# A hybrid decoder layer on one core: recurrence work moved between VectorE, ScalarE and GpSimd

## The chip, the cores and the metric

One core of a Trainium2 chip runs the whole kernel, a single launch. The metric is device time in microseconds (us) of one execution. The engines are TensorE (PE in the profile), VectorE (DVE), ScalarE (ACT), GpSimd (POOL) and SyncE (SP), which here only issues DMAs.

## What is computed

One inference step of one decoder layer, for 512 prompt tokens and 64 new tokens of 8 sampled sequences, 576 token columns in all. On the normalised input two mixers run side by side, a recurrent one (RWKV-7, 8 heads of 64) and a sparse attention (8 heads, 2 key/value heads); then gates, an output projection, a SwiGLU feed-forward network of width 2816 and a last normalisation. The change lies in the recurrent mixer, cut here to its core:

```python
def rwkv7_time_mix(p, prev_row, S0, lp):
    shifted = concat([prev_row[:, None, :], p[:, :-1]], axis=1)      # token shift
    xs = p + (shifted - p) * lp['mu']
    r, wlo, k, v, alo, glo = split(xs)
    w = -softplus(-(lp['w0'] + tanh(wlo) @ lp['w_decay'])) - 0.5
    decay = exp(-exp(w))
    a = sigmoid(lp['a0'] + alo @ lp['w_aaa'])
    kk = normalised(k * lp['k_k'])                                    # per head
    k_h = k * (1 + (a - 1) * lp['k_a'])
    y, S = rwkv7_scan(S0, r, decay, k_h, v, -kk, kk * a)
    ...
    return out, p[:, -1], S                                           # last row: the new shift state

def rwkv7_scan(S0, r, decay, k, v, a_vec, b_vec):                     # per token:
    S = S * w_t + (S @ a_t) b_t^T + v_t k_t^T ;  y_t = S @ r_t
```

## The kernel before

Tokens lie along the columns, features along the 128 partitions. Every projection in full precision is three TensorE passes: weights and activations are split into a rounded part (`whi`, `hh`) and a remainder (`wlo`, `hl`), and `mm3` (L354) adds hi·hi, hi·lo and lo·hi. ScalarE makes `whi` and VectorE makes `wlo` for each tile of 128 output columns (`wsplit`, L334), two buffers of each. A projection tile is 48 matmuls into two PSUM banks (`pd`), which ScalarE empties: into `pe` (L407) for a column tile of the recurrent mixer, into `nsp` or `gate` buffers for the rest.

The recurrent mixer works on four pairs of heads. For pair i, `shifted` makes the token-shifted tiles `k`, `r` and `v`: GpSimd subtracts neighbouring columns of `pe` (L411), VectorE corrects the samples' first columns from `shT` (L412) and blends (L413), and a copy of nine columns (L414) keeps the last rows for the output, in `so`. `rw_operands` makes decay sums and their exponentials (`th`, `cum`, `en`, `ec`, `em`), the normalised key (`kk`) and the in-context rate (`a`), and from them the operands of the chunks (`ag`, `bk`, `gb`, `bt`, all in the tile `state`). `rw_inverse` inverts triangular blocks by 15 elimination steps on VectorE (`invt`, `iw`) with DMAs on either side; `rw_merge_inverse` and `rw_fold_inverse` finish that with many small matmuls. `rw_chain` then walks 8 chunks of 64 tokens in order. For each chunk TensorE multiplies the state `sv` (L803, into `qy`), the state decayed by `lam` is made (`sl`, a slot of the tile `cct`, L806), VectorE copies the first product over `sv` (L807), TensorE multiplies again (L812) and VectorE adds product and decayed state into the next chunk's `sv`. `rw_samples` does the 8 sampled sequences.

Between these steps `pull` puts projection matmuls, so that TensorE has work while a pair's chain waits. The order of instructions on each engine is chosen by a scheduler from a model of the engines' times, with the chain at high priority; it is fixed when the kernel is built, and each engine then runs its own queue strictly in that order. So an edit of one instruction can move many others. After the recurrence come the attention heads (`ns_head`, with L1184, L1195 and L1199) and, from 660 us on, merge, output projection and feed-forward.

Of the kernel before, what the change touches and what calls it, by code (L numbers as in the profile page):

```python
# [16 lines left out]
AF = mybir.ActivationFunctionType  # L17
ALU = mybir.AluOpType
# [90 lines left out]
def tile_hybrid_step(ctx: ExitStack, tc: tile.TileContext, I: dict, O: dict):  # L109
# [3 lines left out]
    V = nc.vector  # L113
    A = nc.scalar
    G = nc.gpsimd
# [29 lines left out]
    def PS(tag, name="ps"):  # L145
        return psum.p.tile([128, 512], F32, name=nm(name), tag=f"b{next(banks[tag])}", bufs=1)
# [4 lines left out]
    def dma(out, in_, eng=None):  # L151
        (eng or nc.sync).dma_start(out, in_)  # L152

    def tt(e, out, a, b, op):
        return e.tensor_tensor(out, a, b, op)  # L155

    def bc(ap, shape):
        return ap.to_broadcast(shape)
# [9 lines left out]
    ident, vec, dvec, cst = base.t(128, "ident"), base.t(64, "vec"), base.t(16, "dvec"), base.t(4, "cst")  # L168
# [4 lines left out]
    def C(cols=NTOK, name="c", dt=F32):  # L173
        return base.t(592, name, "c", 3, dt)[:, 0:cols]
# [14 lines left out]
    def narrow(tag, name, cols=NTOK, dt=F32):  # L189
        p = held if tag in ("o4", "o5", "o6", "o7") else slots  # L190
        return p.t(NTOK, name, tag, 1, dt)[:, 0:cols]
# [11 lines left out]
    shT, so = base.t(15 * 8, "shT"), base.t(15 * 9, "so")  # L203
# [27 lines left out]
    V_W0, V_A0, V_KK, V_KA, V_RK, V_LNW, V_LNB = (31 + 4 * i for i in range(7))  # L231
# [29 lines left out]
    def vc(i):  # L261
        return vec[:, i:i + 1]
# [117 lines left out]
    def proj(pieces, evac):  # L380

        ws = ahead.pop(pieces[0][0], None) or wcols(w_in, pieces, raw=early.pop(pieces[0][0], None))
        for a in range(2):
            pt = PS("pd", "pd")
            for k in range(8):
                mm3(pt, ws[k:k + 1], hx[k:k + 1], cut(a), k == 0, k == 7)
                yield
            evac(cut(a), pt[:, 0:cut(a).stop - cut(a).start])
# [11 lines left out]
    def shifted(pieces, ti, new, then):  # L400
        pe = []

        def evac(c, pt):
            if not pe:
                pe.append(C(577, name="pe"))
                G.memset(pe[0][:, 0:1], 0.0)
            A.copy(pe[0][:, 1 + c.start:1 + c.stop], pt)  # L407
        yield from proj(pieces, evac)
        pe, x = pe[0], new()
        cur = pe[:, 1:577]  # L410
        tt(G, x, pe[:, 0:576], cur, ALU.subtract)  # L411
        tt(V, x[:, T:NTOK:8], shT[:, ti * 8:ti * 8 + 8], cur[:, T:NTOK:8], ALU.subtract)  # L412
        V.scalar_tensor_tensor(x, x, vc(16 + ti), cur, ALU.mult, ALU.add)  # L413
        V.tensor_copy(so[:, ti * 9:ti * 9 + 9], pe[:, 512:577:8])  # L414
        then(x, pe)

    def lora_decay(x, pe):
# [40 lines left out]
    def need(*key):  # L458
        while key not in have:
            pull(1)  # L460
        return have[key]
# [49 lines left out]
    def rw_operands(S, i):  # L511
        cols = slice(i * 128, i * 128 + 128)
        k = need("k", i)
        kk, k2 = narrow("o1", "kk"), narrow("o2", "k2")
# [4 lines left out]
        th, a = narrow("o3", "th"), narrow("o4", "a")  # L519
# [4 lines left out]
        for q, name in ((slice(0, 64), "rwkv_w_decay"), (slice(64, 128), "rwkv_w_aaa")):  # L524
            dma(raw[q], I[name][0][:, cols])
            c = slice(q.start * 2, q.start * 2 + 128)
            for q2 in (slice(0, 64), slice(64, 128)):
# [4 lines left out]
                 lambda c, z: A.activation(th[:, c], z, AF.Tanh, bias=dvec[:, i:i + 1], scale=0.5))  # L532
        small_mm([(w[:, 128:256], la), (w[:, 384:512], la)],
                 lambda c, z: A.activation(a[:, c], z, AF.Tanh, bias=dvec[:, 4 + i:5 + i], scale=0.5))
        G.tensor_scalar(th, th, 1.0, None, ALU.add)
        cum, en = narrow("o5", "cum"), narrow("o6", "en")
        V.tensor_tensor_scan(cum, scanm, th, 0.0, ALU.mult, ALU.add)
        tt(G, th, cum, th, ALU.subtract)
        G.tensor_scalar(a, a, 0.5, 0.5, ALU.mult, ALU.add)
        A.activation(en, cum, AF.Exp, scale=KAPPA)  # L540
        ec, em = cum, th
        A.activation(ec, cum, AF.Exp, scale=-KAPPA)
        A.activation(em, th, AF.Exp, scale=-KAPPA)
        G.tensor_scalar(kk, k, vc(V_KK + i), None, ALU.mult)
        A.activation(k2, k2, AF.Ln, scale=2.0 ** 20)
        A.activation(k2, k2, AF.Exp, bias=c_ln, scale=-0.5)
        tt(V, kk, kk, k2, ALU.mult)
        G.tensor_scalar(k2, a, vc(V_KA + i), dvec[:, 8 + i:9 + i], ALU.mult, ALU.add)
        kh, ba = k, a
        tt(G, kh, k2, k, ALU.mult)  # L550
        tt(G, ba, kk, a, ALU.mult)
# [13 lines left out]
        for h in range(2):  # L565
# [9 lines left out]
            lam = S["lam"][0:64, h]  # L575
# [194 lines left out]
    def gate_weights(i, after):  # L770
        cols = slice(i * 128, i * 128 + 128)
        wg, w1 = slots.t(256, "wgate", "wg1"), slots.t(128, "w1", dt=F32R)
        dma(wg[:, 0:128], I["rwkv_w_gate"][0][0:128, cols])
        dma(wg[0:32, 128:256], I["rwkv_w_gate"][0][128:160, cols])
        for q in (slice(0, 32), slice(32, 64)):
            behind(A.copy(w1[q], wg[0:32, 128:256]), after)
        tt(V, w1[64:96], wg[0:32, 128:256], f(w1[0:32]), ALU.subtract)
        G.memset(f(w1[96:128]), 0.0)
        return wg, w1

    def rw_chain(S, i):
        ag, gb, bt, sv, lam = (S[x] for x in ("ag", "gb", "bt", "sv", "lam"))
        par, ct = S["par"], S["ct"]
        G.memset(sv[0:64, 0], 0.0)
        yb = S["yb"].rearrange("p (j x) -> p j x", x=128)

        cct = slots.t(640, "cct", f"cc{par}")
        ccs = cycle([cct[:, x * 128:x * 128 + 128] for x in range(5)])

        def cc(name):  # L790
            return next(ccs)

        def two(ap):
            return ap.rearrange("p (h i) -> p h i", i=64)

        for c in range(8):
            if c == 4:
                wg, w1 = gate_weights(i, out)

            qy = PS(ct, f"qy{i}c{c}")  # L800
            with tc.high_priority():
                for h in range(2):
                    i_ = MM(qy[:, h * 64:h * 64 + 64], lhsT=ag[h][:, c], rhs=sv[:, c, h], start=h == 0, stop=True, skip_group_check=True)  # L803
                sl = cc("sl")
                sl3 = two(sl[0:64])
                tt(G, sl3, sv[0:64, c], bc(lam[0:64, :, c:c + 1], [64, 2, 64]), ALU.mult)  # L806
                V.tensor_copy(sv[0:64, c], two(qy[0:64, 0:128]))  # L807
            anchor[0] = i_
            pull(PULL[i])
            with tc.high_priority():  # L810
                for h in range(2):
                    i_ = MM(qy[:, 128 + h * 64:192 + h * 64], lhsT=S["btgb"][:, c, h], rhs=sv[:, c, h], start=False, stop=True,  # L812
                            skip_group_check=True)
                pn = two(qy[0:64, 128:256])
                if c < 7:
                    tt(V, sv[0:64, c + 1], pn, sl3, ALU.add)
                else:
                    fin = cc(f"fin{i}")
                    tt(V, two(fin[0:64]), pn, sl3, ALU.add)
                yo = yb[(c % 2) * 64:(c % 2) * 64 + 64, c // 2]  # L820
                out = A.copy(yo, qy[64:128, 0:128])
                tt(V, yo, qy[64:128, 128:256], yo, ALU.add)
            anchor[0] = i_
            pull(PULL[i])
        rw_samples(S, i)

        pf = PS(ct)
        TR(pf[:, 0:64], fin[0:64], ident[0:64, 0:64])
        fo = cc("fo")
        A.copy(fo[:, 0:64], pf[:, 0:64])  # L830
        dma(O["p_rwkv"][0, 0][2 * i:2 * i + 2].rearrange("h i j -> (h i) j"), fo[:, 0:64])

        st = slots.t(32, "gnst", "gnst", 2)
        y3 = yb.rearrange("p j (h i) -> p (j h) i", i=64)
        V.tensor_reduce(st[:, 0:10], y3, AX.X, ALU.add)
        V.tensor_scalar(st[:, 0:10], st[:, 0:10], -1.0 / 64, None, ALU.mult)
        tt(V, y3, y3, bc(st[:, 0:10, None], [128, 10, 64]), ALU.add)
        sq = slots.t(640, "gnsq", "ye")
        A.activation(sq.rearrange("p (j x) -> p j x", x=128), yb, AF.Square)
        V.tensor_reduce(st[:, 10:20], sq.rearrange("p (h i) -> p h i", i=64), AX.X, ALU.add)  # L840
        G.tensor_scalar(st[:, 10:20], st[:, 10:20], 1.0 / 64, GN_EPS, ALU.mult, ALU.add)
        tt(G, st[:, 20:30], st[:, 10:20], npow[:, 0:10], ALU.pow)
        tt(V, y3, y3, bc(st[:, 20:30, None], [128, 10, 64]), ALU.mult)

        p2, pt = PS(ct), PS(ct)
        TR(p2[:, 0:64], yb[0:64, 4], ident[0:64, 0:64])
        for j in range(4):
            TR(pt[:, j * 128:j * 128 + 128], yb[:, j], ident)
        y = slots.t(640, f"yT{i}", "ye")[:, 0:NTOK]
        A.activation(y[:, 0:T], pt, AF.Identity, bias=vc(V_LNB + i), scale=vc(V_LNW + i))  # L850
        A.activation(y[:, T:NTOK], p2[:, 0:64], AF.Identity, bias=vc(V_LNB + i), scale=vc(V_LNW + i))
        tt(G, y, y, yr[i], ALU.add)
        small_mm([(wg[:, 0:128], g0), (w1, g1)],
                 lambda c, pg: tt(V, yr[i][:, c], y[:, c], pg, ALU.mult), ct)
# [903 lines left out]
```

## Time and profile before

| | us |
|---|---|
| median of 3 runs | 1197.24 (1189.47 to 1200.94) |
| profiled execution, its own time | 1198.96 |
| its span, first to last instruction | 1197.2 |
| TensorE clock granted, mean share of full speed | 0.964 |

A profile is one execution. Busy time is the union of an engine's instructions. An idle time in brackets, [us <-who], is that of the engine just before the instruction, and whose result ended it. Lines such as L155 belong to helpers (a two-operand operation), so the tile names tell what an instruction is for. The granted clock is 1.00 at 2.4 GHz and 0.50 at 1.2 GHz.

### The profile page before, as it was taken

How to read it: one execution, taken by the hardware profiler on the slowest of the kernel's cores; microseconds unless marked ns; L12 is line 12 of the kernel's file. 1: busy time of each engine (PE TensorE's matmuls, PEld its weight loads, DVE VectorE, ACT ScalarE, POOL GpSimd, SP SyncE). 2: the span in 40 equal slices, each digit the busy share in tenths (PEclk: the TensorE clock that was granted, in tenths of full speed). 3: DMA queues.
4: the chain of work that ended last, by engine and by line, in shares of the span. 5: the costliest groups of instructions: out<-in, count | busy, mean ns of one | idle time of the engine just before them, and what ended most of it. 6: DMA issues, size and time to landing. Idle time of an engine off the chain costs nothing.

```text
span 1197.2 us, 23170 instructions
## 1 busy us (share of the span) xinstructions
PE 1139.2 (95%) x9117; PEld 1074.5 (90%) x9117; DVE 738.0 (62%) x1444; ACT 509.8 (43%) x1065; POOL 280.8 (23%) x361
## 2 busy tenths in 40 slices
PE   6989899999999989999999999999999999999995
PEld 5989799998888989777787899999999999999995
DVE  5684835359594561786668655698555763367554
ACT  5443533353433422576677433484223341233232
POOL 3443312146244131543237112201000010001000
PEclk9999999999987878999999999999999999999998
DMA  6323334212253242423240653313323243132222
GB/s 181 90 57 81 79 79 105 67 40 68 70 146 87 75 123 69 123 66 98 84 129 3 187 151 94 108 53 109 113 64 95 81 122 91 54 88 71 89 71 80
DMA packets 194791, 108.94 MB, mean 91 GB/s; under 512 B 49780, under 2 KB 187970, under 8 KB 194682
## 3 DMA queue, kind: packets, MB, share of 16 engines
q1 hardware_dynamic: 194682, 107.46, 32.0%
q8 instruction: 72, 1.18, 0.4%
q14 instruction: 37, 0.30, 0.1%
HBM read 91.40 MB, written 16.02 MB: 90 GB/s over the span
## 4 chain that ended last, share of the span: by engine, by line
PE 78%; DVE 11%; ACT 4%; issue 3%; DMA 2%; POOL 2%; SPq 1%; POOLq 0%; ACTq 0%; DVEq 0%
PE pd L359 46%; PE pu L359 9%; PE ps L704 2%; PE acc L1214 2%; PE ps L581 1%; PE ps L1035 1%; PE pT L1199 1%; DVE wlo L155 1%; PE ps L696 1%; PE pS L1184 1%; SPq L152 1%; DVE lo L155 1%; PE sm L396 1%; PE pTs L1308 1%; DMA vtok<-in_cache_slc_kv 1%
## 5 line engine op out<-in xcount | busy, mean ns | idle before, releaser
L359 PE MATMUL pd<-hh,whi 128*128 128x256 f32 (+1 forms) x656 | 206.2, 314 | 5.4 <-ACT pe L407 3.4
L359 PE MATMUL pd<-hh,wlo 128*128 128x256 f32 (+1 forms) x656 | 202.8, 309 | 5.1 <-DVE wlo L155 4.3
L359 PE MATMUL pd<-hl,whi 128*128 128x256 f32 (+1 forms) x656 | 202.7, 309 | 0.0
L359 PE MATMUL pd<-act,hi 128*128 128x288 f32 (+2 forms) x704 | 141.8, 296 | 0.0
L359 PEld LDWEIGHTS pd<-hh,whi 128*128 128x128 f32 x656 | 129.9, 198 | 8.8 <-ACT pe L407 4.4
L359 PEld LDWEIGHTS pd<-hh,wlo 128*128 128x128 f32 x656 | 129.9, 198 | 6.9 <-DVE wlo L155 4.6
L359 PEld LDWEIGHTS pd<-hl,whi 128*128 128x128 f32 x656 | 129.9, 198 | 1.4
L359 PEld LDWEIGHTS pd<-act,hi 128*128 128x128 f32 x704 | 112.6, 188 | 0.1
L359 PE MATMUL pd<-act,lo 128*128 128x288 f32 (+2 forms) x352 | 103.8, 296 | 0.0
L359 PE MATMUL pd<-h2l,hi 128*128 128x288 f32 x352 | 103.6, 295 | 0.0
L359 PE MATMUL pd<-h2h,hi 128*128 128x288 f32 x352 | 103.1, 295 | 0.0
L359 PE MATMUL pd<-h2h,lo 128*128 128x288 f32 x352 | 103.1, 294 | 0.0
L155 DVE TENSOR_TENSOR wlo<-wraw,whi 128x1024 fp32r<-128x1024 f32 x60 | 79.8, 1331 | 37.6 <-ACT whi L337 35.5
L337 ACT CAST whi<-wraw 128x1024 fp32r<-128x1024 f32 x59 | 61.8, 1047 | 93.5 <-PE pd L359 61.1
L155 POOL TENSOR_TENSOR sg<-sg,ut 128x576 f32<-128x576 f32 x11 | 18.1, 1645 | 340.0 <-DVE ut L155 325.3
L337 ACT CAST hi<-wraw 128x1024 fp32r<-128x1024 f32 (+1 forms) x46 | 46.5, 1012 | 117.4 <-PE pd L359 62.6
L155 DVE TENSOR_TENSOR x<-x,pd 128x288 f32<-128x288 f32 (+1 forms) x64 | 28.8, 451 | 65.2 <-PE pd L359 65.2
L155 DVE TENSOR_TENSOR lo<-wraw,hi 128x1024 fp32r<-128x1024 f32 (+1 forms) x46 | 56.9, 1239 | 18.7 <-ACT hi L337 18.6
L359 PEld LDWEIGHTS pd<-h2l,hi 128*128 128x128 f32 x352 | 66.1, 188 | 0.0
L359 PEld LDWEIGHTS pd<-act,lo 128*128 128x128 f32 x352 | 66.1, 188 | 0.0
L359 PEld LDWEIGHTS pd<-h2h,lo 128*128 128x128 f32 x352 | 66.0, 188 | 0.0
L359 PEld LDWEIGHTS pd<-h2h,hi 128*128 128x128 f32 x352 | 65.9, 188 | 0.0
(540 smaller groups left out, 2964.8 us busy)
## 6 DMA issues: line engine op xcount, KB each, us to landing
wraw<-in_w_in SPq DMA_DIRECT2D x35, 512.0 KB
wraw<-in_w_ffn_gate SPq DMA_DIRECT2D x22, 512.0 KB
ur<-in_w_ffn_up SPq DMA_DIRECT2D x44, 256.0 KB
wraw<-in_w_ffn_down SPq DMA_DIRECT2D x16, 512.0 KB
gt<-gsp SPq DMA_DIRECT2D x16, 288.0 KB
xt<-in_x_prompt SPq DMA_DIRECT2D x8, 512.0 KB
wraw<-in_w_out SPq DMA_DIRECT2D x8, 512.0 KB
wraw<-in_w_ffn_down SPq DMA_DIRECT2D x8, 384.0 KB
```

The source lines that it names most:

```text
L152: (eng or nc.sync).dma_start(out, in_)
L155: return e.tensor_tensor(out, a, b, op)
L337: e[0](hi[:, 0:n], raw[:, 0:n])
L359: i_ = MM(pt[:, 0:w_], lhsT=w, rhs=x[:, c], start=first and k == 0 and j == 0, stop=last and k == n - 1 and j == 2, **kw)
L396: MM(pt[:, 0:HALF], lhsT=l, rhs=r[:, half(a)], start=i == 0, stop=i == len(terms) - 1)
L581: MM(pt[:, c * 128:(c + 1) * 128], lhsT=bk[0:64, c0 + c], rhs=ag[:, c0 + c], start=True, stop=True)
L696: TR(pt[0:64, c * 128:c * 128 + 128], S["ag"][h][:, c0 + c, 0:64], ident)
L704: MM(pw[:, x * 64:x * 64 + 64], lhsT=S["at"][h][:, c], rhs=S["gb"][64:128, c, h], start=True, stop=True)
L1035: MM(po, lhsT=w[:, sl_], rhs=z[:, l, :, hf:hf + 162], start=hf == 0 and l == 0 and j == 0, stop=hf == 1 and l == 7 and j == 2)
L1184: MM(pS[:, 0:nk], lhsT=qs[:, qt * 128:qt * 128 + 128], rhs=kh[:, 0:nk], start=True, stop=False, skip_group_check=True)
L1199: TR(pT[:, kt * 128:kt * 128 + 128], P[:, kt * 128:kt * 128 + 128], ident)
L1214: MM(po[:, c0:hf * 256 + 256], lhsT=lv, rhs=ptx[m][:, kk * 256 + q0:kk * 256 + 256], start=name == "slc" and hf == 0 and kt == 0 and j == ...
```

## The change

Three moves between engines; the arithmetic stays the same. The decayed state `sl` of each chunk (32 instructions) goes from GpSimd to VectorE. Four scalings per pair of heads (16 instructions: `th` plus one, `a` to a half of itself plus a half, `k` times a column, `a` times a column plus a column) go from GpSimd to ScalarE. The 15 nine-column copies into `so` go from VectorE to ScalarE.

```diff
@@ shifted
         V.scalar_tensor_tensor(x, x, vc(16 + ti), cur, ALU.mult, ALU.add)
-        V.tensor_copy(so[:, ti * 9:ti * 9 + 9], pe[:, 512:577:8])
+        A.copy(so[:, ti * 9:ti * 9 + 9], pe[:, 512:577:8])
@@ rw_operands
-        G.tensor_scalar(th, th, 1.0, None, ALU.add)
+        A.activation(th, th, AF.Identity, bias=1.0)
...
-        G.tensor_scalar(a, a, 0.5, 0.5, ALU.mult, ALU.add)
+        A.activation(a, a, AF.Identity, bias=0.5, scale=0.5)
...
-        G.tensor_scalar(kk, k, vc(V_KK + i), None, ALU.mult)
+        A.mul(kk, k, vc(V_KK + i))
...
-        G.tensor_scalar(k2, a, vc(V_KA + i), dvec[:, 8 + i:9 + i], ALU.mult, ALU.add)
+        A.activation(k2, a, AF.Identity, bias=dvec[:, 8 + i:9 + i], scale=vc(V_KA + i))
@@ rw_chain
-                tt(G, sl3, sv[0:64, c], bc(lam[0:64, :, c:c + 1], [64, 2, 64]), ALU.mult)
+                tt(V, sl3, sv[0:64, c], bc(lam[0:64, :, c:c + 1], [64, 2, 64]), ALU.mult)
```

The scheduler makes a new order from it; up to the merge, every engine's queue is affected. Three places follow, before and then after.

ScalarE, first pair of heads, from the second half of `a` to the emptying of the next projection tile (`pe` from `pd_1008`; `whi_1167` are weights for a tile after it). Before:

```order
L534 ACTIVATE a_615<-sm_640,dvec_65 128x288
L528 CAST wl_1067<-wr_1066 64x128 x4
L540 ACTIVATE en_646<-cum_645 128x576
L337 CAST whi_1167<-wraw_1165 128x1024
L407 COPY pe_1005<-pd_1008 128x320
L542 ACTIVATE cum_645<-cum_645 128x576
L543 ACTIVATE th_614<-th_614 128x576
L407 COPY pe_1131<-pd_1045 128x256
```

After:

```order
L540 ACTIVATE en_646<-cum_645 128x576
L534 ACTIVATE a_615<-sm_640,dvec_65 128x288
L528 CAST wl_1067<-wr_1066 64x128 x4
L539 ACTIVATE a_615<-a_615 128x576
L542 ACTIVATE cum_645<-cum_645 128x576
L543 ACTIVATE th_614<-th_614 128x576
L548 ACTIVATE k_115_600<-a_615,dvec_65,vec_64 128x576
L337 CAST whi_1167<-wraw_1165 128x1024
L407 COPY pe_1005<-pd_1008 128x320
L414 COPY so_108<-pe_1005 128x9
L407 COPY pe_1131<-pd_1045 128x256
```

Between `en` and the emptying of `pd_1008` stood one cast; now a half of `a`, four small casts, two of the moved scalings and two exponentials stand there as well.

VectorE, around the end of the second pair's samples (`state` from `qy1c`, L752, which a matmul of the samples waits for), amid the elimination steps of the third pair. Before:

```order
L155 TENSOR_TENSOR iw_319<-iw_319,invt_3123 36x2x13x3
L155 TENSOR_TENSOR invt_3123<-iw_319,im_318 36x56
L155 TENSOR_TENSOR wlo_4404<-wraw_4401,whi_4403 128x1024
L155 TENSOR_TENSOR iw_319<-iw_319,invt_3123 36x2x14x2
L155 TENSOR_TENSOR state_317<-r_456_3352,cum_3958 64x4x64
L155 TENSOR_TENSOR state_317<-r_456_3352,cum_3958 64x5x64
L752 COPY state_317<-qy1c_500_3672 64x128
```

After:

```order
L155 TENSOR_TENSOR iw_319<-iw_319,invt_3123 36x2x12x4
L155 TENSOR_TENSOR wlo_4404<-wraw_4401,whi_4403 128x1024
L155 TENSOR_TENSOR invt_3123<-iw_319,im_318 36x78
L752 COPY state_317<-qy1c_500_3672 64x128
L155 TENSOR_TENSOR iw_319<-iw_319,invt_3123 36x2x13x3
```

The copy now stands ahead of the last two elimination steps and of the two products with `cum`.

GpSimd, from the spreading of the samples' queries (`qbr`, `qbu`) to the first attention probabilities (`P`). Before:

```order
L1116 TENSOR_SCALAR qbu_5898<-qraw_5894 64x8x8 x2
L778 MEMSET w_750_5509 32x128
L1116 TENSOR_SCALAR qbu_5898<-qraw_5896 64x8x8 x2
L155 TENSOR_TENSOR cct_5415<-state_317,lam_3911 64x128
L1195 TENSOR_SCALAR P_5927<-P_5927,ast_5237,gt_75 128x128
```

After:

```order
L1116 TENSOR_SCALAR qbu_5898<-qraw_5894 64x8x8 x2
L155 TENSOR_TENSOR yT_699_5048<-yT_699_5048,yr_81 128x576
L778 MEMSET w_750_5509 32x128
L1195 TENSOR_SCALAR P_5927<-P_5927,ast_5237,gt_75 128x128
L1195 TENSOR_SCALAR P_5940<-P_5940,ast_5237,gt_75 128x256
```

The decayed state has left the queue; the third pair's output sum `yT` has moved in front of the first probabilities, and the last two spreadings stand further back.

## Rows read from the trace of the kernel before

**Rows 1.** Page, engines: busy us (share of the span) and instructions.
```profile
PE 1139.2 (95%) x9117; PEld 1074.5 (90%) x9117; DVE 738.0 (62%) x1444; ACT 509.8 (43%) x1065; POOL 280.8 (23%) x361
```
**Rows 2.** TensorE's timeline: five matmuls that began after idle time, in brackets.
```profile
81.00 0.51 PE L396 MATMUL sm<-k,bones 128*128 128x288 f32 x1 [2.20 <-DVE k L554]
...
87.47 0.30 PE L562 MATMUL ps<-ident,v 128*64 128x128 f32 x1 [1.71 <-DVE yr L155]
...
146.81 0.39 PE L359 MATMUL pd<-hh,wlo 128*128 128x256 f32 x1 [4.34 <-DVE wlo L155]
...
342.23 0.36 PE L754 MATMUL qy1c<-state 64*64 64x64 f32 x1 [2.85 <-DVE state L752]
...
428.30 0.47 PE L812 MATMUL qy2c<-state 128*128 128x64 f32 x1 [3.29 <-DVE state L807]
```
**Rows 3.** Instruction groups by shape: count, busy us, mean ns, idle before, releaser.
```profile
L155 POOL TENSOR_TENSOR cct<-state,lam 64x128 f32<-64x128 f32 x32 | 19.2, 599 | 87.6 <-DVE state L155 78.8 <-PE ps L671 6.9 <-DVE so L414 1.3
L535 POOL TENSOR_SCALAR th<-th 128x576 f32<-128x576 f32 x4 | 7.4, 1859 | 15.2 <-ACT th L532 15.2
L544 POOL TENSOR_SCALAR kk<-k,vec 128x576 f32<-128x576 f32 x4 | 6.9, 1727 | 3.2 <-DVE k L413 3.2
L548 POOL TENSOR_SCALAR k<-a,vec,dvec 128x576 f32<-128x576 f32 x4 | 3.5, 879 | 0.3
L539 POOL TENSOR_SCALAR a<-a 128x576 f32<-128x576 f32 x4 | 3.5, 878 | 0.0
L1116 POOL TENSOR_SCALAR qbr<-qr 64x64 f32<-64x64 f32 x8 | 5.4, 675 | 0.5
L1116 POOL TENSOR_SCALAR qbu<-qraw 64x64 f32<-64x64 f32 x8 | 3.4, 421 | 0.5
L543 ACT ACTIVATE th<-th 128x576 f32<-128x576 f32 x4 | 2.7, 674 | 0.9 <-POOL th L155 0.9
L528 ACT CAST wl<-wr 64x128 fp32r<-64x128 f32 x16 | 4.7, 295 | 0.2
L414 DVE COPY so<-pe 128x9 f32<-128x9 f32 x15 | 12.3, 817 | 0.0
L807 DVE COPY state<-qy2c 64x128 f32<-64x128 f32 x8 | 2.3, 283 | 14.4 <-PE qy2c L803 14.3
L807 DVE COPY state<-qy0c 64x128 f32<-64x128 f32 x8 | 2.3, 282 | 5.5 <-PE qy0c L803 5.4
```
**Rows 4.** Timeline of the first pair's operands, 65 to 74 us.
```profile
65.99 1.12 DVE L414 COPY so<-pe 128x9 f32<-128x9 f32 x1
...
67.11 0.67 DVE L155 TENSOR_TENSOR v<-shT,pe 128x8 f32<-128x8 f32 x1
...
67.32 0.50 ACT L534 ACTIVATE a<-sm,dvec 128x288 f32<-128x288 f32 x1 [0.73 <-PE sm L396]
...
69.33 1.28 POOL L539 TENSOR_SCALAR a<-a 128x576 f32<-128x576 f32 x1
70.05 2.15 DVE L155 TENSOR_TENSOR wl<-wr,wl 64x128 fp32r<-64x128 f32 x2
70.17 0.69 ACT L540 ACTIVATE en<-cum 128x576 f32<-128x576 f32 x1 [1.23 <-DVE cum L537]
...
70.76 1.04 ACT L337 CAST whi<-wraw 128x1024 fp32r<-128x1024 f32 x1
71.70 0.42 ACT L407 COPY pe<-pd 128x320 f32<-128x320 f32 x1
...
73.25 0.35 ACT L407 COPY pe<-pd 128x256 f32<-128x256 f32 x1
```
**Rows 5.** Windows: stretch, length, busy us (count) per engine, clock, DMA share, GB/s.
```profile
342.00:348.80 6.80, 6.57 (x32) 6.46 (x32) 6.67 (x18) 1.75 (x3) 0.00 (x0) 0.50 0.77 214
...
376.10:400.00 23.90, 23.90 (x127) 21.38 (x128) 5.20 (x19) 6.75 (x15) 6.76 (x12) 0.50 0.13 29
400.00:427.30 27.30, 25.00 (x297) 24.10 (x295) 23.01 (x49) 11.47 (x26) 8.79 (x7) 1.00 0.42 112
```

## The prediction

> **What bounds the kernel now.** I read the engine table first: TensorE is busy for 95% of the span, and no edit touches its work [rows 1]. From 660 us to the end its projections run without a gap worth naming, so the change can only matter before. There I asked what TensorE waits for: its timeline, looking only at matmuls that begin after idle time. The five longest such waits between 60 and 498 us add up to 14.4 us (2.20 + 1.71 + 4.34 + 2.85 + 3.29), and all five end on VectorE [rows 2]. That is the first thing to see: VectorE, in the stretches where a pair's operands and inverse are made, is what is late; GpSimd matters as far as VectorE waits for it or is held up beside it. The second thing is the clock. For 23.9 us from 376 us on TensorE was granted 0.50, 1.2 GHz, and did 127 matmuls there, against 297 in the 27.3 us after it at 2.4 GHz; VectorE was busy for only 5.2 of those 23.9 us, so here TensorE's own slow clock was the limit [rows 5].
>
> **The decayed state** (32 instructions) leaves GpSimd, where one took 599 ns on average, and joins VectorE. A similar VectorE operation on 64x128, the copy at L807, takes 282 ns [rows 3], so 9.0 us of VectorE are added. On the path they cost nothing: the copy that follows waits for TensorE's product (L803) anyway, 14.4 us in eight chunks of the third pair, and in the first pair still 5.5 us in eight, 0.69 us a chunk, more than 0.28 [rows 3]. If that cover were gone the whole 9.0 us would show. The GpSimd version was seldom late, so I book 0, with -1 and +9 as ends.
>
> The rows show VectorE held up by GpSimd: two 64x128 operations took 2.15 us together beside two GpSimd instructions at 69 to 72 us [rows 4], where 0.28 each would do. The Trainium skill (SBUF — State Buffer, section Who interferes with whom) says that a VectorE instruction with two inputs in SBUF blocks wholly against a GpSimd instruction that reads SBUF; it speaks against this move, because the new product has two such inputs and the copy at L807 has only one, from PSUM. By that rule a part of the 32 would wait out a GpSimd instruction; the trace agrees that such holds exist, and the sum would rise by about 3 us, inside the ends above.
>
> **The nine-column copies** (15) took 12.3 us of VectorE, 817 ns each [rows 3], far more than nine columns need. The row at 65.99 shows why that is not a gain of 12: the copy ended at 67.11 and the next VectorE instruction, the correction of `v`, needs GpSimd's subtraction of the same tile, beside which the copy was held [rows 4]. Without the copy VectorE waits for that instead. I take -0.5, ends 0 and -3. ScalarE pays at most 0.3 us each, the price of a 64x128 cast [rows 3], 4.4 us beside other work.
>
> **The sixteen scalings** took 7.4 + 6.9 + 3.5 + 3.5 = 21.3 us of GpSimd. A ScalarE pass over the same 128x576 takes 674 ns (L543), so ScalarE gets 16 x 0.67 = 10.8 us [rows 3]. Of latency, `th` plus one (1.86 us down to 0.67) stands straight ahead of the decay sum, so that goes 1.2 us earlier in each pair. The other three only clear GpSimd's queue: the product with the scaled `a` comes no earlier, because ScalarE now makes that scaling at the end of a longer queue (below). VectorE is held less: L539 at 69.33 ran beside the slow pair of operations at 70.05 [rows 4]. I book -2 for that, ends 0 and -5, from the 1.6 us lost there (2.15 less twice 0.28), in up to three pairs.
>
> **Where TensorE's waits go.** The waits at 81.00 and 87.47 (3.9 us) end on VectorE work of the first pair. The decay sum comes 1.2 us sooner, the copy at L414 and a weight remainder no longer stand ahead of that work, and VectorE is held less: I let both waits go, -3.9. The wait at 146.81 (4.34) is a weight remainder queued behind elimination steps; the new order only moves the remainder that is late, 0. The wait at 342.23 (2.85) ends on L752, which now stands ahead of two elimination steps and two products: -2.3. For 428.30 (3.29), behind rotary work, I take -2.0: the order there changes, by an amount that I cannot see; its ends are 0 and -3.3 [rows 2].
>
> **What is paid for it.** On ScalarE the emptying of the next projection tile stood 1.53 us after the start of `en` (70.17 to 71.70). In the new order it stands behind half an `a` (0.5), four casts (4 x 0.3), four passes of 0.67 and the weight cast (1.0), with `en` itself 0.7 [rows 3, 4]: 6.1 us, so 4.6 us later, less the 1.2 us by which `en` starts sooner, 3.4. Queued behind it is TensorE, which needs that PSUM bank; it had work until the next emptying at 73.25, that is 1.5 us of cover. So it loses 1.9 us in the first pair, and in the other three I take a third of that each, as their queues differ: +3.8 in all; ends 0 and 4 x 3.4 = +13.6. On GpSimd, the first probabilities waited behind sixteen spreadings (5.4 + 3.4 us) [rows 3]; the decayed state leaves that queue and `yT` enters it ahead: +0.5 for TensorE, which waits for these probabilities either way.
>
> **The sum**, against the profiled execution's own 1198.96: 0 - 0.5 - 2 - 3.9 - 2.3 - 2.0 + 3.8 + 0.5 = -6.4, so 1192.6; the median shown is 1.7 lower than that execution, which is well inside the runs' spread. I predict 1192. A measurement of this kernel tells about 1%, 12 us, from no change.
>
> **Rivals.** First, *ScalarE's queue becomes the bound* (slower). At its upper end above, each pair stalls TensorE by 3.4 us with no cover, and the expected removals do not come, since VectorE's later steps wait for the same exponentials: 1199 + 13.6 = 1213. It decides from the point where the emptying is later than TensorE's other bank lasts, 1.5 us; for the first pair I already expect that, and against it stands that later pairs sit among small matmuls. Second, *the clock* (faster): if the new order keeps TensorE dense through the stretch at 376 to 400, up to half of 23.9 us comes back, and half of the 6.8 us from 342 on [rows 5]: 12 + 3.4 on top of the sum, 1177. Nothing in the edits aims at it, and it may as well go the other way. Third, *the waits only move*: the new queues put other instructions ahead of what TensorE needs, -6.4 comes to nothing, and the time is 1198. The wait at 146.81 is the model for it.
>
> The engine table alone would back this third one. PE is the busiest at 95%, and work goes from the idlest compute engine (POOL 23%) to busier ones, DVE 62% and ACT 43% [rows 1]. The Trainium skill (Perfetto Trace Analysis, section Identifying the Most-Contended Engine) says to optimize the engine with the highest occupancy first; by that rule this change gains nothing, 1199. The waits of rows 2 speak against taking the whole span at once.
>
> **How the numbers follow.** The forecast 0.46; the waits only move 0.20; ScalarE's queue 0.18; the clock 0.16. Of the forecast's own spread (the ends above, and one stretch of low clock more or less, 12 us either way) I put 0.14 below 1185 and 0.02 above 1209. Faster by over 1%: 0.16 + 0.14 = 0.30; slower by over 1%: 0.18 + 0.02 = 0.20; within 1%: 0.50. The range must reach both the clock's and the ScalarE queue's times to leave out 2 in 10: 1172 to 1213.
>
> **What would show it.** Right: no wait of TensorE on L554 or `yr` near 80 to 90 us; no wait on L752 near 340; a wait of 1 to 3 us on the emptying of `pe` (L407) near 75; the decayed state on VectorE at about 0.28 us with the copy L807 still waiting for TensorE; `so` at 0.3 us or less on ScalarE. Wrong: TensorE waiting on L407 or L337 in every pair, more than 5 us in all; new waits on VectorE longer than the five; or a sum of half-clock time that differs by over 20 us from before, which would outweigh all terms here.

## The result, and the profile after

The change made the kernel slower: 1211.85 us median (1209.34 to 1218.63, 4 runs) against 1198.31 (1189.47 to 1200.94), a ratio of 1.0129 with a 95% interval of 1.0087 to 1.0171. The forecast was 1192, range 1172 to 1213. The profiled execution took 1211.96 us, its span 1210.2, at a mean granted clock of 0.950 (0.964 before). Medians here and below are of all runs; the ratios leave out runs over 1.5% above the fastest of their kernel, and two experiments, in which most runs were such, have none.

What the edit does to the engines is as planned. Of the page after, the engines (answers to [rows 1]):

```profile
PE 1152.7 (95%) x9117; PEld 1087.0 (90%) x9117; DVE 729.4 (60%) x1461; ACT 523.3 (43%) x1096; POOL 242.2 (20%) x313
```

VectorE is busy for less time than before in spite of 17 more instructions (32 came, 15 left), GpSimd for 38.6 us less, and no engine but TensorE is near its limit. TensorE has the same 9117 matmuls, and they take 13.5 us longer. The moved instructions after answer to [rows 3]. The decayed state as a group by shape (columns as there):

```profile
L155 DVE TENSOR_TENSOR cct<-state,lam 64x128 f32<-64x128 f32 x32 | 9.0, 280 | 6.2 <-PE ps L671 5.6
```

The others by source line, with minimum, median and maximum in ns, and the first and last start:

```profile
L535 ACT ACTIVATE th<-th x4: 680/698/702, 64.8 to 321.2; 128x576 f32<-128x576 f32 x4
...
L539 ACT ACTIVATE a<-a x4: 667/682/687, 69.7 to 327.9; 128x576 f32<-128x576 f32 x4
...
L544 ACT ACTIVATE kk<-k,vec x4: 757/763/765, 54.2 to 281.5; 128x576 f32<-128x576 f32 x4
...
L548 ACT ACTIVATE k<-a,dvec,vec x4: 852/862/870, 71.4 to 328.7; 128x576 f32<-128x576 f32 x4
...
L414 ACT COPY so<-pe x15: 204/208/214, 30.5 to 286.8; 128x9 f32<-128x9 f32 x15
```

The prices of `sl`, `th` and `a` are close to those used; the scalings with a column for scale, or for scale and bias, took 0.76 and 0.86 us where 0.67 was used, the nine-column copies 0.21 of the 0.3 allowed. TensorE's timeline after, the matmuls that began after idle time where the prediction had looked (to set beside [rows 2]):

```profile
73.60 0.42 PE L359 MATMUL pd<-hh,whi 128*128 128x320 f32 x1 [0.92 <-ACT pe L407]
78.30 0.39 PE L359 MATMUL pd<-hh,wlo 128*128 128x256 f32 x1 [0.68 <-DVE wlo L155]
85.32 1.07 PE L562 MATMUL ps<-ident,v 128*64 128x128 f32 x8 [0.69 <-DVE yr L155]
...
131.61 0.64 PE L359 MATMUL pd<-hh,whi 128*128 128x320 f32 x1 [3.32 <-ACT nsp L887]
...
335.45 0.27 PE L828 MATMUL ps<-ident,cct 64*128 64x64 f32 x1 [2.08 <-DVE so L155]
...
416.57 0.20 PE L661 MATMUL ps<-invt,state 16*32 16x16 f32 x2 [2.03 <-DMA invt<-d2p]
...
497.39 0.66 PE L812 MATMUL qy3c<-state 128*128 128x64 f32 x4 [2.02 <-DVE state L807]
499.35 0.89 PE L1199 MATMUL pT<-ident,P 128*128 128x128 f32 x2 [0.89 <-DVE yr L155]
```

The waits for L554, L752 and the 4.34 us for `wlo` are gone, that for `yr` is shorter; others have come, and one at 497 stands where none of that length stood.

The decisive reading is a milestone. The first score product of the attention (L1184) comes at 498.9 us before and at 488.7 after, with the same work done on both sides but for twenty instructions in the order. So up to there the changed kernel is **10.2 us ahead** in these two profiles, and behind it it **lost 23**. Windows of the two heads, columns as in [rows 5], before and then after:

```profile
0.00:498.90 498.90, 466.62 (x4126) 435.76 (x4126) 293.74 (x591) 205.40 (x425) 165.97 (x214) 0.93 0.34 90
...
0.00:488.70 488.70, 462.95 (x4116) 433.73 (x4116) 282.42 (x604) 217.46 (x452) 124.91 (x166) 0.93 0.35 92
```

TensorE's idle time in the head (length less busy) fell by 6.5 us, from 32.3 to 25.8. The other 3.7 us are busy time, and no clear gain: some ten matmuls of the last pair's chain and gates now run behind the milestone, about 2 us by their spacing (an estimate). Nor does one profile tell 10 us here: with `sl` alone moved in the old order (below), a kernel whose time is that of before, the first L1184 came at 488.9 in an execution of 1188.83 us.

Windows from the first L1184 to the first turning of the selected pages' keys (L1284), and from there to the last product with the values (L1214); columns as in [rows 5]. Before:

```profile
498.90:547.60 48.70, 43.90 (x318) 35.02 (x318) 39.09 (x110) 34.44 (x104) 28.48 (x47) 0.93 0.30 73
547.60:664.00 116.40, 110.53 (x782) 89.50 (x781) 80.27 (x242) 78.11 (x253) 43.40 (x73) 0.99 0.26 79
```

After, the longest stretch at half clock first, then the two windows:

```profile
499.10:529.80 30.70, 30.45 (x153) 25.70 (x153) 14.51 (x45) 12.40 (x40) 10.65 (x17) 0.50 0.19 47
...
488.70:550.60 61.90, 55.59 (x306) 46.26 (x305) 38.37 (x105) 33.09 (x96) 28.62 (x45) 0.67 0.24 61
550.60:676.80 126.20, 115.93 (x808) 92.67 (x807) 83.33 (x249) 81.25 (x264) 45.28 (x75) 0.97 0.27 81
```

165.1 us before, 188.1 after, for the same work but for those matmuls. From there to the end both take the same time, 533.2 and 533.4 us. TensorE's idle time (length less busy) went from 10.7 to 16.6 us, its busy time from 154.4 to 171.5: some waits, and a clock that stood at 0.50 for 41 of the first 61.9 us (twice 0.33 of the length), 30.7 of them in one piece. None of the 63 moved instructions but the chain's last few stands in this stretch. What changed here is the order, which the scheduler had drawn anew.

### The profile page after: what moved, and what is told of

It is laid out like the page before. It is cut to its first block, busy times and chain, and to the rows that moved or that the text cites. A ratio compares the mean times of both kernels' runs of the same rounds, so it can differ in the third digit from the quotient of the medians.

```text
span 1210.2 us, 23174 instructions
## 1 busy us (share of the span) xinstructions
PE 1152.7 (95%) x9117; PEld 1087.0 (90%) x9117; DVE 729.4 (60%) x1461; ACT 523.3 (43%) x1096; POOL 242.2 (20%) x313
## 4 chain that ended last, share of the span: by engine, by line
PE 79%; DVE 8%; ACT 4%; DMA 4%; issue 2%; POOL 1%; SPq 1%; POOLq 0%; ACTq 0%; DVEq 0%
PE pd L359 47%; PE pu L359 9%; PE acc L1214 2%; PE ps L704 2%; PE ps L581 2%; PE pT L1199 1%; PE ps L1035 1%; PE pS L1184 1%; PE sm L396 1%; PE pq L733 1%; PE ps L696 1%; DVE lo L155 1%; DMA vtok<-in_cache_slc_kv 1%; PE pS L1186 1%; DVE wlo L155 1%
```

## The experiments

The order can be held fixed. The kernels below write the order of each engine out as a table of 11,444 numbers and give each instruction a dependency of order alone, with no wait, on the one that is to stand ahead of it:

```python
for n in seq:                                   # numbers in the order of the code
    i = traced[int(n)]
    e = str(i.engine).split(".")[-1]
    if e in last:
        tc.add_manual_dep(i, last[e].name, dep, reason="order of the engine's work")
    last[e] = i
```

So one can put new engines into an old order, cut between two orders, or move single queue entries. A moved instruction stands, in a foreign order, where it stood in time in that order.

**Engines against order: four runs.** Two theories: the new order costs the time, or the new engines do (ScalarE's queue).

`after_fixed`, the changed kernel with its own table:

```diff
         tile_hybrid_step(tc, ins, outs)
+        pin_order(tc, nc)          # table: the changed kernel's order
```

> The changed kernel with the order of every engine written out as it already was (dependencies of order alone, no wait), so that later runs can move single instructions. Both theories: 1212 us (1208 to 1219), the time of the changed kernel. If the low clock is set by the program, half-clock time is again about 120 us in all, with the long stretch from about 499 to 530 us; if it falls at random, its place is another one and the time may differ by 12 us either way.

1206.03 us (1196.41 to 1217.32, 10 runs), 1.0069 (1.0029 to 1.0110), less than the 1208 to 1219 expected. The profiled execution, 1204.8 us, has no long stretch of half clock behind L1184; that of `after_fixed_again` (below, the same program) has it, from 500.7 to 531.4 us, where the changed kernel had it. So the place is the same, and whether it comes differs between executions.

`new_engines_old_order`: the changed kernel, table of the kernel before.

```diff
+        pin_order(tc, nc)          # changed kernel; table: the order of before
```

> The moved instructions on their new engines, but every other instruction in the order of the kernel before, and the moved ones at the place in time that they had there. Theory 1 (the new order costs the time, through TensorE's stretch from 498 to 550 us and its low clock): 1190 to 1201, as before or a little less, half-clock time 70 to 100 us. Theory 2 (the engines cost it: ScalarE's longer queue and 9 us more of VectorE): 1206 to 1216.

1189.48 us, 0.9962 (0.9931 to 0.9993): faster than before, by a little more than expected. Theory 1.

`old_engines_new_order`: the kernel before, table of the changed kernel.

```diff
+        pin_order(tc, nc)          # kernel before; table: the changed kernel's order
```

> All instructions on the engines of before, in the order of the changed kernel. Theory 1 (order): 1206 to 1216, with a half-clock stretch of 20 us or more between 495 and 550 us. Theory 2 (engines): 1192 to 1201.

1209.01 us, 1.0110 (1.0041 to 1.0180): as slow as the changed kernel without one instruction moved between engines. Theory 1 in both corners: engines -0.4%, order +1.1%. The detail failed: its profile has some 14 us of half clock from L1184 to L1284 (clock 0.87 over 54.3 us), not a stretch of 20.

`after_late_gate`: the wait at 497, traced back, is VectorE's copy L807 behind a remainder of the gate weights, which waits for a cast, which waits for a transfer. Timeline of VectorE after:

```profile
496.74 0.28 DVE L155 TENSOR_TENSOR w<-wgate,w 32x128 fp32r<-32x128 f32 x1 [1.39 <-ACT w L776]
497.06 0.28 DVE L807 COPY state<-qy3c 64x128 f32<-64x128 f32 x1
```

Of ScalarE after:

```profile
496.41 0.62 ACT L776 CAST w<-wgate 32x128 fp32r<-32x128 f32 x2 [2.24 <-DMA wgate<-in_rwkv_w_gate]
```

```diff
-L776 CAST w<-wgate x2                 (ScalarE, ahead of chunk 6)
-L155 TENSOR_TENSOR w<-wgate,w         (VectorE, ahead of chunk 6's L807)
 L807 COPY state<-qy3c                 (chunk 7)
+L776 CAST w<-wgate x2
+L155 TENSOR_TENSOR w<-wgate,w
```

> The changed kernel in its own order, with three instructions moved back: the two casts of the last pair's gate weights on ScalarE (L776) and their remainder on VectorE now stand behind the copy of chunk 7 (L807) and not ahead of that of chunk 6, so that nothing waits for their transfer. The 2.0 us wait of TensorE at 497 goes in any case. Theory 1a (that wait is what is followed by 30 us at half clock): 1195 to 1201, half-clock time between 495 and 550 us under 15 us. Theory 1b (the clock falls in this stretch of small matmuls anyway): 1207 to 1212, and the half-clock stretch stays over 20 us.

1204.23 us, 1.0078 (1.0038 to 1.0118). It decides nothing, because the pause only moved. TensorE's timeline of this run:

```profile
496.67 0.66 PE L812 MATMUL qy3c<-state 128*128 128x64 f32 x4 [0.23 <-DVE state L807]
...
500.42 1.10 PE L1199 MATMUL pT<-ident,P 128*128 128x128 f32 x3 [2.55 <-DVE yr L155]
```

Then 0.50 from 500.2 to 530.9 us. The ten executions fall in two groups, six from 1199.5 to 1204.7 us at a mean clock of 0.955 to 0.961, four from 1212.1 to 1213.5 at 0.948 to 0.950.

**Where in the order: two cuts, and the edits apart.** `new_head_old_tail`: changed kernel, table of its own order to the first L1184, that of before behind it.

```diff
+        pin_order(tc, nc)          # table: new order up to L1184, then the order of before
```

> The changed kernel's engines throughout. Order of every engine: as in the changed kernel up to the first score product of the attention (L1184), which is reached with the same work done but for some twenty instructions, and as in the kernel before from there on. Theory 1c (the new order gains 7 to 10 us up to that point and loses 14 to 23 us behind it): 492 + 697 us of span, so 1186 to 1192 us, faster than before. Theory 1d (the head leaves something behind, so that any order is late behind it): 1200 to 1212.

1191.33 us, 0.9942 (0.9911 to 0.9974). Theory 1c.

`old_head_new_tail`, the reverse:

```diff
+        pin_order(tc, nc)          # table: order of before up to L1184, then the new one
```

> The same cut the other way: the order of before up to the first score product (L1184), the order of the changed kernel from there on, on the changed kernel's engines. Theory 1c: 496 + 711 to 721 us of span, so 1205 to 1219 us, and half-clock time behind the cut above 25 us in some executions. Theory 1d: 1188 to 1194.

1205.72 us, 1.0057 (1.0021 to 1.0093), with 27 us of half clock behind the cut in the profile. Theory 1c again: the loss is in the order behind L1184.

`sl_old_order` and `scalings_old_order`: one part of the change each, the order of before.

```diff
-                tt(G, sl3, sv[0:64, c], bc(lam[0:64, :, c:c + 1], [64, 2, 64]), ALU.mult)
+                tt(V, sl3, sv[0:64, c], bc(lam[0:64, :, c:c + 1], [64, 2, 64]), ALU.mult)
+        pin_order(tc, nc)          # table: the order of before
```

> Only the decayed state moves to VectorE, all else in the order of before. By the prediction's step (its cost is hidden behind TensorE's product): 1194 to 1197, no difference from before. By the rival step (9 us more of VectorE show): 1200 to 1205. If the state's way through the shorter VectorE instruction is the gain: 1189 to 1192.

1194.26 us, 0.9987 (0.9963 to 1.0011): no difference.

```diff
-        G.tensor_scalar(th, th, 1.0, None, ALU.add)
+        A.activation(th, th, AF.Identity, bias=1.0)
...
+        pin_order(tc, nc)          # the other three scalings too; table: the order of before
```

> Only the sixteen scalings move to ScalarE, all else in the order of before. If the gain of the new engines in the old order (0.4%) is mainly theirs (VectorE less held up, the decay sum earlier): 1189 to 1193. If ScalarE's queue takes it back: 1195 to 1201.

1188.71 us, 0.9929 (0.9896 to 0.9961). The gain of the new engines is the scalings'; the nine-column copies were not tried alone.

**The scheduler's own orders, and a third cut.** `sl_own_order` is the first of these two edits without the table:

```diff
-        pin_order(tc, nc)
```

> Only the decayed state moves to VectorE, in the order that the scheduler makes of it. With the order of before the same kernel took 0.9987 of the time of before, so what is different here is order alone. If any edit redraws the order and the time with it: outside 1190 to 1198. If the costly order comes from the changed kernel's scalings or copies: 1190 to 1198.

1211.59 us (1191.85 to 1218.71, 6 runs). The same edit cost nothing in the old order; here the spread alone is 27 us, and the median is that of the changed kernel. Its order behind L1184 is almost the changed kernel's: matched by line, tiles and shape in the traces, some 35 of VectorE's 857 instructions there stand elsewhere, against some 265 when it is compared with before. Its two windows (table below) are 49.4 and 125.3 us. So moving the decayed state alone makes the scheduler draw the costly tail. What that costs in all stays open here: one of the six ran at 1191.85.

`scalings_own_order`, likewise:

```diff
-        pin_order(tc, nc)
```

> Only the sixteen scalings move to ScalarE, in the scheduler's own order; with the order of before they gave 0.9929. If the scheduler's answer to the scalings is what costs: 1200 to 1212, with waits behind the first score product as in the changed kernel. If not: 1185 to 1193.

1193.25 us (1177.38 to 1203.27, 12 runs), 0.9947 (0.9908 to 0.9986). The scalings get an order of their own, unlike both others behind L1184, and it costs nothing measurable.

`new_order_to_pages`: cut at the first L1284.

```diff
+        pin_order(tc, nc)          # table: new order up to L1284, then the order of before
```

> The changed kernel with its own order up to the first turning of the selected pages' keys (L1284, about 542 to 550 us) and the order of before from there on; the cut at the first score product gave 1191, the order of the changed kernel throughout 1206 on the same chip. Theory 1e (about 6 us of the loss are waits behind this point, the rest is the wait for probabilities and low clock ahead of it): 1194 to 1203. If all of it lies ahead: 1204 to 1210. If all of it lies behind: 1189 to 1193.

1199.47 us, 1.0016 (0.9989 to 1.0042), as theory 1e has it: by the ratios some 9 us of the loss lie between the two cuts (0.9942 to 1.0016) and 6 behind the second (to 1.0069; 11 by the 1.0108 of the same program below).

`scalings_new_head_old_tail`, an attempt at a better version:

```diff
+        pin_order(tc, nc)          # scalings alone; table: new order up to L1184, then before
```

> A version that takes what gained: only the scalings move, the order of the changed kernel up to the first score product, that of before behind it. If the gains of engines and head add up: 1180 to 1188. If the head's gain is the same microseconds as the scalings': 1188 to 1192, as either alone.

1191.61 us, 0.9964 (0.9937 to 0.9992): faster than before, but the gains don't add up. The scalings in the old order have the lowest time of the versions tried, though not clear of noise: the intervals of all five that beat the kernel before overlap.

**Loads or compute queues.** `new_order_old_loads`:

```diff
+        pin_order(tc, nc)          # new order; SyncE behind L1284: the order of before
```

> The changed kernel in its own order; only the transfer queue (SyncE) is in the order of before from the first turning of the selected pages' keys (L1284) on. From that point to the last product with the values (L1214) orders of before took 114 to 116 us, new orders 125 to 130. If the order of the loads makes that: 114 to 118 us there, and about 1196 to 1200 for the whole. If the compute engines' order makes it: 124 to 130 us there, and 1203 to 1210.

1203.89 us, 1.0060 (1.0024 to 1.0096), and 126.4 us from L1284 to the last L1214: the compute engines' order (a part of it is work moved, see the table below). `old_order_new_loads`:

```diff
+        pin_order(tc, nc)          # new order up to L1284, then before; SyncE: new order
```

> The same cut the other way: from L1284 on the four compute engines in the order of before, the transfer queue in that of the changed kernel; ahead of it all as in the changed kernel. If the loads: 124 to 130 us from L1284 to the last L1214, 1203 to 1210 in all. If the compute engines' order: 114 to 118 us, 1196 to 1202.

1214.51 us (1190.73 to 1218.66, 6 runs; it has the long stretch of half clock ahead of the cut), and 120.0 us behind the cut, between the two expectations. The loads' order can cost some 5 us beside old compute queues (114.6 in `new_order_to_pages`), in waits of TensorE on `vtok`, 5.9 us against 1.6. With the new compute queues old loads save little: those waits are 1.8 us in `new_order_old_loads`, 2.8 in the changed kernel, 1.6 before.

**The pause.** `after_no_pause` moves the gate weights of the last pair as above, and of GpSimd's sixteen spreadings twelve, which stood ahead of `yT` and the first probabilities:

```diff
-L1116 TENSOR_SCALAR qbr<-qr x6, qbu<-qraw x6
 L155 TENSOR_TENSOR yT<-yT,yr
 L1195 TENSOR_SCALAR P<-P,ast,gt       (the first eight)
 L155 TENSOR_TENSOR s0t<-s0t,lam       (the second)
+L1116 TENSOR_SCALAR qbr<-qr x6, qbu<-qraw x6
```

> The changed kernel in its own order, with two things moved that made TensorE pause for 2 to 2.6 us at 495 to 500 us: the three instructions on the last pair's gate weights as in the run before, and twelve of GpSimd's sixteen spreadings (L1116), which now stand behind the first eight probabilities and the sums for the samples. No pause over 1 us is left between 490 and 502 us. Theory 2a (the long stretch of half clock that began at 499 to 502 us is started by that pause): half-clock time from the first score product to L1284 under 15 us, no executions in a group 10 us above the others, 1197 to 1203. Theory 2b (it comes in this order without the pause too): about 4 executions in 10 some 10 us longer, median 1202 to 1208.

`after_fixed_again` is `after_fixed` once more, with the same edit, beside it on the same chip:

> The changed kernel once more, beside the last one on the same chip. Theory 2b: medians within 4 us of each other. Theory 2a: this one 4 to 10 us longer, 1203 to 1210.

1199.90 us, 1.0034 (1.0010 to 1.0059), beside 1211.48 us, 1.0108 (1.0066 to 1.0149), for the same kernel with the pause: the intervals don't meet, and no group lies apart (1195.1 to 1207.3). That is as theory 2a has it, within limits: the first measurement of the program with the pause, 1.0069 (1.0029 to 1.0110) on another chip, does overlap, and fifteen instructions were moved, not the pause alone. TensorE's timeline without the pause:

```profile
494.68 0.66 PE L812 MATMUL qy3c<-state 128*128 128x64 f32 x4 [0.46 <-DVE state L807]
496.31 0.52 PE L1199 MATMUL pT<-ident,P 128*128 128x128 f32 x3 [0.43 <-POOL P L1195]
503.96 0.60 PE L716 MATMUL ps<-ident,s0n 64*64 64x64 f32 x8 [1.50 <-DVE vcat L155]
```

Its two windows:

```profile
487.50:541.40 53.90, 46.77 (x305) 38.18 (x304) 38.90 (x105) 32.56 (x96) 27.89 (x45) 0.84 0.28 70
541.40:668.50 127.10, 116.47 (x810) 94.13 (x807) 83.42 (x249) 81.42 (x264) 45.29 (x75) 0.97 0.26 80
```

The first window of the kernel with the pause:

```profile
490.20:552.30 62.10, 55.56 (x305) 46.23 (x304) 38.41 (x105) 33.05 (x96) 28.70 (x45) 0.67 0.24 61
```

The two pauses at 495 to 500 are nearly gone (0.46 and 0.43 us). A later one of 1.50 us has come at 504, with 13.7 us of half clock behind it (17 in this window, more than the 15 expected). The 127.1 us behind are what every new order has.

The same windows for all profiles:

| order behind L1184 | kernel | L1184 to L1284, us (clock) | to the last L1214 |
|---|---|---|---|
| old | before | 48.7 (0.93) | 116.4 |
| old | `new_engines_old_order` | 48.4 (0.93) | 115.1 |
| old | `new_head_old_tail` | 49.3 (0.97) | 115.0 |
| old | `sl_old_order` | 48.8 (0.90) | 114.8 |
| old | `scalings_old_order` | 49.7 (0.93) | 114.4 |
| new | after | 61.9 (0.67) | 126.2 |
| new | `after_fixed` | 49.8 (0.93) | 126.7 |
| new | `after_fixed_again` | 62.1 (0.67) | 126.1 |
| new | `old_engines_new_order` | 54.3 (0.87) | 129.8 |
| new | `old_head_new_tail` | 56.0 (0.76) | 128.5 |
| old | `scalings_new_head_old_tail` | 52.5 (0.90) | 115.4 |
| new, two entries later | `after_late_gate` | 62.0 (0.67) | 125.6 |
| new, without the pauses | `after_no_pause` | 53.9 (0.84) | 127.1 |
| `sl`'s own | `sl_own_order` | 49.4 (0.90) | 125.3 |
| scalings' own | `scalings_own_order` | 49.1 (0.86) | 119.1 |
| new, old from L1284 | `new_order_to_pages` | 67.3 (0.70) | 114.6 |
| new, old loads from L1284 | `new_order_old_loads` | 49.1 (0.93) | 126.4 |
| new, old compute from L1284 | `old_order_new_loads` | 67.5 (0.70) | 120.0 |

The last column goes with the order, whatever the engines, the head or the clock ahead: 114 to 116 for the old, 125 to 130 for the new, `sl`'s own with them, the scalings' own and the mixed one between. But the two columns don't hold the same work in both orders: TensorE does 318 and 782 matmuls in them before, 306 and 808 after, because the new order does one group of scores behind L1284. About 4 us of the step in the last column are that work (an estimate from the spacing of such matmuls), and only the sum of the columns compares like with like. Waits are a part of that step too: TensorE's idle time in the last column is 5.9 us before and 10.3 after. The column before it goes with the clock in the main.

## Why the prediction was wrong, point by point

**The step that failed** isn't the sentence on the end of the program, which held: from the last L1214 on both kernels take the same time. It is what was left out before that: "There I asked what TensorE waits for" went up to 498 us, and the 160 us between that and the merge stand in the sum as one term, "+0.5 for TensorE, which waits for these probabilities either way", with the clock at 0. The runs show 11.4 us (`after_fixed`: 49.8 + 126.7 against 48.7 + 116.4) to 23 us (after) lost just there, about 2 us of each the matmuls moved there. In `after_fixed` most of it is TensorE waiting, 18.4 us idle against 10.7; after, 5.9 us are, and most of the rest is the clock. The order does it: on the same engines, `old_head_new_tail` took 1.0057, `new_engines_old_order` 0.9962. That the order differs up to the merge at 660 us was known; the prediction takes three places of it, and behind 490 GpSimd's alone.

At GpSimd's place "either way" was wrong. Before, TensorE reached the first turning of probabilities (L1199) without a wait:

```profile
509.07 0.86 PE L1199 MATMUL pT<-ident,P 128*128 128x128 f32 x3
```

After, `yT` stood in front of the first probabilities behind the spreadings, as the order showed, and TensorE waited 0.89 us at 499 (the profile puts it down to VectorE's `yr`, which waits for `yT`; the first `P`, from 498.72 on GpSimd, came late as well). What came with it in that profile is 30.7 us at 1.2 GHz.

**The clock** I booked at 0 with 12 us either way, and gave it a rival only on the fast side, since "Nothing in the edits aims at it, and it may as well go the other way". It went the other way, and the last of the signs named for being wrong came true: half-clock time, by the mean clocks and spans, was about 86 us before and 121 after (twice the share of the clock that wasn't granted, times the span). `after_no_pause` makes it likely that part of this hangs on the pauses that the order makes. That rival should have stood on both sides.

**The head of the program was right in sum.** -6.4 was forecast; the first L1184 came 10.2 us earlier in this profile, 6.8 and 8.7 in the two others of the same program, 6.5 of the 10.2 in less waiting. Over whole executions, the new engines with the new head and the old tail gave -0.58% (-0.26 to -0.89), about -7 us of 1196, and on the old order throughout -0.38% (-0.07 to -0.69), -4.5 us. That the sum fits is luck in part, because its terms missed both ways. Term by term:
- The decayed state, 0: right. All 32 instructions took 271 to 285 ns, and 0.9987 is no difference. The Trainium skill (SBUF — State Buffer, section Who interferes with whom) has a VectorE instruction with two inputs in SBUF contend with a GpSimd instruction that reads SBUF. Only three of the 32 ran beside such a GpSimd instruction, and they took 271 to 284 ns, so this case hardly tests the rule.
- The scalings, -2 and the waits that go: -0.71% alone, -8.5 us (-4.7 to -12.4), as much as all three moves together gave in that order, or more. The two 64x128 operations that had taken 2.15 us beside GpSimd [rows 4] now take 0.59.
- The copies, -0.5: not tried alone; 208 ns on ScalarE, as said.
- TensorE's waits: those on L554, L752 and L807 (428 us) went, as forecast or further, that on `yr` in part (0.69 left). The 4.34 us behind the inverse went as well, which I had at 0. In their place came 3.32 us on the emptying of `nsp` (1.58 before), 2.08 on `so`, 2.03 and 1.09 on `invt`. The third rival, that the waits only move, holds for a part of them.
- ScalarE's queue, +3.8: too large. The emptying of `pe` came 1.4 us later (73.13 against 71.70), not 3.4, mainly because `en` started 2.7 us sooner (67.47 against 70.17), not 1.2; TensorE waited 0.92 us there. The waits on L407 of over 0.4 us add up to 4.7 us (0.46 + 1.36 + 1.04 + 0.92 + 0.94), 3.4 before (0.46 + 1.36 + 1.04 + 0.58): +1.3. The first rival, that this queue becomes the bound, falls: with the new engines in the old order the kernel is faster.

**The size.** 1211.85 lies beside that rival's 1213 and within the range, for another reason, so that is luck as well.

## What to carry to other kernels

Where a scheduler draws the order, an edit is two changes: the instructions that it moves, and a new order for all the others. Judge them apart, by holding the order fixed by hand: here the engines gave -0.4%, the order +1.1%, and the lowest time came from a part of the edit in the old order (0.9929). In a prediction, look at every stretch where the order differs, not only at where the edited lines run, and look there for entries that wait for a transfer or sit behind a row of bulk work, ahead of something that TensorE needs.

## What was not expected of the hardware

- A short pause of TensorE can be followed by a long stretch at 1.2 GHz although it is busy: idle for 2.02 and 0.89 us at 495 to 499, then 0.50 for 30.7 us in which it was busy for 30.45. But a pause isn't enough: in `after_fixed` 3.50 us at the same place were followed by 3.4 us at half clock (502.6 to 506.0):

```profile
502.24 0.86 PE L812 MATMUL qy3c<-state 128*128 128x64 f32 x4 [3.50 <-DVE state L807]
```

Set side by side, the 18 profiles show more. The stretch of 30.7 us stands in the five in which TensorE waited 0.83 to 2.55 us for the first probabilities (L1199): the changed kernel, `after_fixed_again`, `after_late_gate`, `new_order_to_pages` and `old_order_new_loads`; the clock fell within 0.3 us of that wait's end. It stands in no other, though in five of those TensorE waited 2.58 to 4.68 us on L807 near there, beside 3.4 to 10.2 us at half clock. Why that wait and not the longer one stays open.
- One program in one order (`after_fixed`) gave 1196.4 to 1217.3 us, the ten executions at mean clocks from 0.967 down to 0.946; the scalings in the old order stayed within 1181.3 to 1195.4, at 0.975 to 0.963.
